# Two output tiles on LRU and S5 rows traced ahead of the end of the SSD stage, and half of w_out's SSD rows in another pool

## The chip, the cores and the metric

One core of one Trainium2 chip runs the whole program. The time is the device time of one execution in microseconds (us), as the median over runs. The engines are TensorE (PE, matmuls, with its weight loads as PEld), VectorE (DVE), ScalarE (ACT), GpSimd (POOL) and SyncE (SP), whose queue issues the DMAs here. Each engine works through its own instructions in a fixed order.

## What is computed

One step of a hybrid recurrent decoder layer, for 2048 prompt tokens and 64 sample tokens of width 1024:

```python
h = rmsnorm(x, norm_g) @ w_in            # split into z, xBC, dt, LRU, S5 columns
ssd = rmsnorm(ssd_scan(silu(conv(xBC)), dt, ...) * silu(z), ssd_norm_g)   # 16 heads, 4 groups, chunks of 128
lru = rg_lru(conv(...)) * gate           # 512 wide
s5  = glu(gelu(s5_scan(...))) * gate     # 512 wide
out = x + concat([ssd, lru, s5]) @ w_out # 2048 mix columns -> 1024
y   = rmsnorm(out, final_norm_g)
```

The outputs are y and the new states. All of it is held to float32 accuracy.

## The kernel before

The residual x is held on chip in four segments of 512 tokens and one of 64 sample tokens, each as two 16-bit tiles XH and XL (a high and a low part, 8 KB a partition) in the pool `xpool`, tag "xs", eight buffers. A float32 product is made as three 16-bit matmuls, high by high, high by low, low by high, with PSUM adding them up; `in_proj` (L247 to L249) does this for one block of 128 columns and one segment.

The stages follow one another: S5, LRU, and then SSD in four groups g = 0 to 3, each with the segments in the order 0, 1, (2, 4), 3. Within a segment there are four chunks of 128 tokens. A chunk needs the scores e (L524 to L531), its own y (L568 on e, L571 on the state hst carried from the chunk before), and its contribution to the state (L573, then hst L577 and L578). DVE adds y to x (L582), gates it (L655), and the rows go to a buffer `ysp` in the chip's memory (L383). Chunks 12 to 15, of segment 3, come last in a group. All rows of LRU and S5 were written to `ysp` long before.

The output stage multiplies the 2048 rows of y by w_out, 16 blocks of 128 rows: blocks 0 to 7 for SSD, 8 to 15 for LRU and S5. `w_out_rows` loads a block through a staging tile wo32 (two of them, L1144), takes a square sum on ACT (L1148) and small powers of two on DVE, and splits it into high and low on ACT (L1154) and DVE (L1155); two blocks share a tile `wo`. `w_out_scale` then finds one common scale for eight blocks, with a small matmul into ps_sc (L168), and rescales the tiles on DVE (L1168). `load_yt` reads 256 tokens of eight blocks' rows (y, L1182) and splits them into yt on ACT (L1186) and DVE (L1187). `out_part` makes 2 x 8 x 3 = 48 matmuls of 128x512 (L1175 to L1177) for a tile of 128 tokens, in two halves, each added into `res` by DVE (L1195).

The SSD rows need a norm over all of them: sqacc gathers their squares (L662), matmuls with ones sum them (L1302, L1303), and rstd and u0 follow. So for the first six tiles (NPRE) the LRU and S5 part comes first, 288 matmuls; then u0 is computed, and the rest of the tiles follows with both parts.

What sets the order on each engine is a scheduler that simulates the traced program: instructions are traced in the order of the code and are then placed by when they could start. Tiles get memory by pool: the output stage's pool `oa` takes the place of the SSD working pool (closed by `done` in the last segment of group 3), and `ob` takes the place of the pool `ssx`, closed by `sA.close()` after the last SSD row. Blocks are prepared as tiles of "xs" come free, which is during the last SSD group.

The functions around the change, with the lines that the profile names:

Of the kernel before, what the change touches and what calls it, by code (L numbers as in the profile page):

```python
# [8 lines left out]
F32 = mybir.dt.float32  # L9
F16 = mybir.dt.float16  # L10
# [32 lines left out]
def hymba_step_kernel(  # L43
# [577 lines left out]
                V.tensor_tensor(hv, hv, ps, op=ALU.add)  # L621
            S.dma_start(out=o_ssd_s[g, :, 4 * q:4 * q + 4], in_=hb)

    def ssd_group(sx, sp, g, done):
        blks = [2 * g, 2 * g + 1, 8 + g, 12 + g]
        ws = [WB[c0] for c0 in SB(g)]
        rows = [Row(k, unz[:, k:k + 1] if k < ZE else WB[k]) for k in (2 * g, 2 * g + 1)]
        tls = [Tail(b) for b in blks]
        H = None

        def channels(i, s):

            w, un, _ = ws[i]
            b = blks[i]
            raw = conv_raw(in_proj(w, s), un, s, tls[i], stS[:, b, :])
            if s == 3:
                w_ahead()
            x = seg_tile("xxbc"[i] + str(i % 2), "x", s, sx if i < 2 else sp, SG, 5 if i < 2 else 2)
            conv(x, raw, s, [col("sconv_w", 16 * j + b, hcols) for j in range(4)], col("sconv_b", b, hcols))
            th = seg_tile("th", "th", s, st)  # L640
            A.activation(out=th, in_=x, func=AF.Tanh)  # L641
            V.scalar_tensor_tensor(x, th, 1.0, x, op0=ALU.add, op1=ALU.mult)
            return x

        def gated(j, s, y):
            k = 2 * g + j
            s0, n = SEGS[s]
            if k < ZE:
                pz = seg_tile("pz", "pz", s, st)
                S.dma_start(out=pz, in_=zb[k, :, s0:s0 + n])  # L650
            else:
                pz = gate(in_proj(WB[k][0], s), WB[k][2], s)
                if s == 3:
                    w_ahead()
            V.tensor_tensor(y, y, pz, op=ALU.mult)  # L655
            if g == 0 and j == 0:
                sqacc[s] = sx.tile([128, SEGS[s][1]], F32, name="sqacc", tag=f"sqacc{s}", bufs=1)
                rows[j].add(s, y, sqacc[s])
            else:
                sq = sx.tile([128, SG], F32, name="sq", tag="sq", bufs=2)[:, :SEGS[s][1]]  # L660
                rows[j].add(s, y, sq)
                G.tensor_tensor(sqacc[s], sqacc[s], sq, op=ALU.add)  # L662

        for segs in SSD_ORD:
            xb = {s: [] for s in segs}
            for i in range(4):
                for s in segs:
                    xb[s].append(channels(i, s))
            for s in segs:
                x0, x1, BT, CT = xb[s]  # L670
                if s == 4:
                    ssd_sample(sp, g, (x0, x1), BT, CT)
                else:
                    for c in range(4 * s, 4 * s + 4):
                        H = ssd_chunk(sp, g, (x0, x1), BT, CT, c, H)
            if 3 in segs:
                S.dma_start(out=o_ssd_p[g], in_=H)
                done()
            for j in range(2):
                for s in segs:  # L680
                    gated(j, s, xb[s][j])


    t9 = const.tile([128, 4, 9], F32, name="t9")
# [449 lines left out]
    def w_out_rows(k0, nk):  # L1134


        tiles = []
        rb = tmp.tile([128, 8], F32, name="rb", tag="rb", bufs=3)
        for k in range(k0, k0 + nk):
            if (k - k0) % 2 == 0:  # L1140
                wo = xpool.tile([128, 2, 2, D], F16, name="wo", tag="xs")
            tiles.append(wo[:, (k - k0) % 2])
            w = wp.tile([128, D], F32, name="wo32", tag="w32", bufs=2)
            S.dma_start(out=w, in_=w_out[k * 128:(k + 1) * 128, :])  # L1144
            m = tmp.tile([128, 1], F32, name="o_m", tag="o_m")
            r = tmp.tile([128, 1], F32, name="o_r", tag="o_r", bufs=4)
            ng = col("ssd_norm_g", k) if k < 8 else 1.0
            A.activation(out=tiles[-1][:, 1, :].bitcast(BF16), in_=w, func=AF.Square, scale=ng, accum_out=m)  # L1148
            root_exponent(m, m)
            pow2_bits(r, m, 204)  # L1150
            pow2_bits(rb[:, k - k0:k - k0 + 1], r, 254)
            if k < 8:
                V.tensor_scalar(r, r, ng, None, op0=ALU.mult)
            A.activation(out=tiles[-1][:, 0, :], in_=w, func=AF.Copy, scale=r)  # L1154
            V.scalar_tensor_tensor(tiles[-1][:, 1, :], w, r, tiles[-1][:, 0, :], op0=ALU.mult, op1=ALU.subtract)  # L1155
        return tiles, rb
# [19 lines left out]
            P.matmul(ps, lhsT=h, rhs=w[:, 1, c], start=False, stop=False)  # L1176
            P.matmul(ps, lhsT=l, rhs=w[:, 0, c], start=False, stop=(k == nk - 1))  # L1177

    def load_yt(k0, t0, n):

        r = oa.tile([128, 8, 256], F32, name="y32", tag="y32", bufs=2)
        S.dma_start(out=r[:, :, :n], in_=ysp[k0:k0 + 8, :, t0:t0 + n].rearrange("k p t -> p k t"))  # L1182
        hl = (oa if k0 else ob).tile([128, 8, 2, 256], F16, name="yt", tag=f"yt{k0}", bufs=2)
        for k in range(8):
            c = rsc[:, k0 + k:k0 + k + 1]
            A.activation(out=hl[:, k, 0, :n], in_=r[:, k, :n], func=AF.Copy, scale=c)  # L1186
            V.scalar_tensor_tensor(hl[:, k, 1, :n], r[:, k, :n], c, hl[:, k, 0, :n], op0=ALU.mult, op1=ALU.subtract)  # L1187
        return [(hl[:, k, 0, :], hl[:, k, 1, :]) for k in range(8)]

    def out_part(tiles, yt, un, n, o, res):  # L1190
        for hf in range(2):
            c = slice(512 * hf, 512 * hf + 512)
            ps = bank(pmm, "mm", "ps_o")[:n]
            out_half(tiles, yt, n, o, ps, c)
            V.scalar_tensor_tensor(res[:n, c], ps, un, res[:n, c], op0=ALU.mult, op1=ALU.add)  # L1195
# [13 lines left out]
    def out_res(t0, n):  # L1209
        res = wp.tile([128, D], F32, name="res", tag="whl")  # L1210
        S.dma_start(out=res[:n], in_=x[t0:t0 + n])
        return res
# [7 lines left out]
    def pool(stack, name, side, bufs=1):  # L1220
        return stack.enter_context(tc.tile_pool(name=name, bufs=bufs, side=side, reuse_waits="tile"))
# [67 lines left out]
    sA, sB = ExitStack(), ExitStack()  # L1289
    sx = pool(sA, "ssx", "left")  # L1290
    sp = pool(sB, "ssw", "right", 2)
    for g in range(4):
        ssd_group(sx, sp, g, sB.close if g == 3 else (lambda: None))
    oq = ExitStack()
    oa = pool(oq, "outa", "right")
    rstd = const.tile([128, 17], F32, name="rstd")
# [12 lines left out]

    ob = pool(oq, "outb", "left")  # L1310
    NPRE = 6
    w1, rb1 = w_out_rows(8, 8)
    u1 = w_out_scale(w1, rb1, 8)
    w0, rb0 = w_out_rows(0, 8)
    pre = []
    for i in range(NPRE):
        if i % 2 == 0:
            yt1 = load_yt(8, 128 * i, 256)
        pre.append(out_res(128 * i, 128))
        out_part(w1, yt1, u1, 128, 128 * (i % 2), pre[i])  # L1320
    u0 = w_out_scale(w0, rb0, 0)
    rsu = tmp.tile([128, 17], F32, name="rsu", tag="rsu", bufs=1)
    V.tensor_scalar(rsu, rstd, u0, None, op0=ALU.mult)
    fg = ob.tile([128, D], F32, name="fg")
    S.dma_start(out=fg, in_=final_g.unsqueeze(0).to_broadcast([128, D]))
    fgs = ob.tile([128, 512], F32, name="fgs")
# [117 lines left out]
```

## Time and profile before

| | |
|---|---|
| median of 3 runs | 1679.58 us (1679.41 to 1679.8) |
| the profiled execution | 1682.5 us, span 1680.8 us |
| mean granted clock of PE | 0.971 |
| PE busy | 1587.2 us, 94% of the span, 9474 instructions |
| DVE, ACT, POOL busy | 1112.0, 858.2, 540.9 us |
| output matmuls (L1175 to L1177) | 3 x 512, 584.6 us |
| in_proj matmuls (L247 to L249) | 3 x 1280, 1474.6 us, overlapped with one another |

The profile is one execution of the program on the chip. A row of the timeline gives the start and the length of an operation (or of several alike) and, in brackets, how long its engine had been idle before it and what ended that. Matmuls follow each other faster than the length of one, because they are pipelined: their pace is read from starts. The granted clock of PE is a share of its full 2.4 GHz, so 0.50 is the level of 1.2 GHz. The stretch of interest is the last fifth: the SSD stage ends near 1319 us, the output stage runs to the end.

### The profile page before, as it was taken

Reading aid. Unit: us, or ns where it says so; the run is one execution under the profiler, and the core shown is the slowest. Engines: PE = TensorE matmul, PEld = TensorE weight load, DVE = VectorE, ACT = ScalarE, POOL = GpSimd, SP = SyncE. Lnnn points to the kernel's source line nnn. Section 1 sums busy time; section 2 is a strip of 40 time slices with the busy share of each in tenths; the row PEclk is TensorE's granted clock in tenths of the full one; section 3 lists DMA queues with packets and bytes.
Section 4 is the critical chain, followed back from the end, with each engine's and each line's share of the span. In section 5 each row is a group of like instructions: output and inputs, shape, how many; then the busy total and the mean of one; then the engine's idle time right before and its main releaser. Section 6 shows DMA issues by size and latency. Waiting matters only on the chain.

```text
span 1680.8 us, 26643 instructions
## 1 busy us (share of the span) xinstructions
PE 1587.2 (94%) x9474; PEld 820.9 (49%) x9474; DVE 1112.0 (66%) x2643; ACT 858.2 (51%) x1913; POOL 540.9 (32%) x822
## 2 busy tenths in 40 slices
PE   6899899898988999999999999999999799999998
PEld 3554544444434444455555555555555444444443
DVE  7844578997476665688878966687777725543332
ACT  7823434443697776666566646566765412322210
POOL 1213226774032111164557645454554100000000
PEclk9999799998989999999999999999999699999999
DMA  7412322322333442433434433242335522633100
GB/s 244 131 48 51 105 95 92 90 89 84 98 90 110 118 140 75 114 94 88 149 109 122 151 104 105 58 155 91 117 114 189 164 75 76 200 101 100 45 25 32
DMA packets 143942, 178.18 MB, mean 106 GB/s; under 512 B 66424, under 2 KB 92480, under 8 KB 143808
## 3 DMA queue, kind: packets, MB, share of 16 engines
q1 hardware_dynamic: 143808, 176.47, 34.4%
q8 instruction: 75, 1.23, 0.3%
q14 instruction: 59, 0.48, 0.1%
HBM read 126.57 MB, written 48.69 MB: 104 GB/s over the span
## 4 chain that ended last, share of the span: by engine, by line
PE 44%; DVE 7%; DMA 3%; ACT 3%; issue 2%; POOL 2%; SPq 0%; POOLq 0%; ACTq 0%; DVEq 0%
PE ps_o L1175 7%; PE ps_o L1176 7%; PE ps_o L1177 7%; PE ps_mm L248 5%; PE ps_mm L247 5%; PE ps_mm L249 5%; DVE x L355 3%; PE ps_y L568 1%; PE ps_s L573 1%; PE ps_y L571 1%; DMA ce<-eT 1%; PE ps_s L618 1%; DMA wo<-in_w_out_dram 1%; DVE e L531 1%; PE ps_tp L545 1%
## 5 line engine op out<-in xcount | busy, mean ns | idle before, releaser
L247 PE MATMUL ps_mm<-xh,whl 128*128 128x512 f16 x1280 | 492.0, 384 | 11.1 <-DVE pz L363 7.3
L249 PE MATMUL ps_mm<-xh,whl 128*128 128x512 f16 x1280 | 491.0, 384 | 0.9 <-DVE whl L206 0.9
L248 PE MATMUL ps_mm<-xl,whl 128*128 128x512 f16 x1280 | 491.6, 384 | 0.0
L248 PEld LDWEIGHTS <-whl 128*128 128x128 f16 x1600 | 155.6, 99 | 161.0 <-issue 29.4
L247 PEld LDWEIGHTS <-whl 128*128 128x128 f16 x1600 | 159.0, 101 | 145.3 <-issue 15.2
L249 PEld LDWEIGHTS <-whl 128*128 128x128 f16 x1600 | 156.1, 99 | 150.7 <-issue 14.2
L1175 PE MATMUL ps_o<-wo,yt 128*128 128x512 f16 x512 | 195.1, 381 | 5.2 <-ACT yt L1186 3.0
L355 DVE SCALAR_TENSOR_TENSOR x<-raw,hcols,x 128x512 f32<-128x512 f32 x192 | 173.6, 904 | 38.1 <-ACT x L353 35.9
L1176 PE MATMUL ps_o<-wo,yt 128*128 128x512 f16 x512 | 195.3, 381 | 0.0
L1177 PE MATMUL ps_o<-wo,yt 128*128 128x512 f16 x512 | 194.2, 380 | 0.0
L1186 ACT ACTIVATE yt<-y,rsc 128x256 f16<-128x256 f32 (+1 forms) x144 | 56.7, 477 | 109.9 <-PE ps_o L1177 81.1
L524 ACT ACTIVATE e<-bcq,acum 128x128 f32<-128x128 f32 (+1 forms) x272 | 85.7, 386 | 35.0 <-PE ps_y L568 32.7
L1347 ACT ACTIVATE yo<-res 128x1024 f32<-128x1024 f32 x16 | 16.8, 1049 | 154.6 <-DVE res L1195 154.5
L538 POOL TENSOR_TENSOR ce<-ce,x 128x512 f32<-128x512 f32 x60 | 81.5, 1364 | 42.5 <-DMA ce<-eT 34.3
L641 ACT ACTIVATE th<-x 128x512 f32<-128x512 f32 x64 | 40.1, 627 | 100.9 <-DVE x L355 100.6
L1195 DVE SCALAR_TENSOR_TENSOR res<-ps_o,rsu,res 128x512 f32<-128x512 f32 x32 | 24.0, 750 | 95.1 <-PE ps_o L1177 95.1
L1175 PEld LDWEIGHTS <-yt 128*128 128x128 f16 x512 | 50.4, 98 | 64.0 <-ACT yt L1186 3.3
L1176 PEld LDWEIGHTS <-yt 128*128 128x128 f16 x512 | 50.3, 98 | 63.1 <-issue 3.5
L363 DVE SCALAR_TENSOR_TENSOR pz<-th,ps_mm 128x512 f32<-128x512 f32 x64 | 43.6, 682 | 55.2 <-ACT th L362 54.7
L1177 PEld LDWEIGHTS <-yt 128*128 128x128 f16 x512 | 50.3, 98 | 60.9 <-issue 0.6
L531 DVE TENSOR_TENSOR e<-e,gm 128x512 f32<-128x512 f32 (+1 forms) x68 | 57.2, 841 | 28.5 <-POOL gm L530 23.8
L362 ACT ACTIVATE th<-ps_mm,sc_out 128x512 f32<-128x512 f32 x64 | 43.7, 682 | 61.9 <-PE ps_mm L249 61.3
(449 smaller groups left out, 3029.3 us busy)
## 6 DMA issues: line engine op xcount, KB each, us to landing
w<-in_w_blk_dram SPq DMA_DIRECT2D x40, 512.0 KB
bcq<-aT SPq DMA_DIRECT2D x64, 256.0 KB
y<-ysp SPq DMA_DIRECT2D x16, 1024.0 KB
ce<-eT SPq DMA_DIRECT2D x60, 256.0 KB
xt<-in_x_dram SPq DMA_DIRECT2D x16, 512.0 KB
ysp<-x SPq DMA_DIRECT2D x32, 256.0 KB
wo<-in_w_out_dram SPq DMA_DIRECT2D x16, 512.0 KB
res<-in_x_dram SPq DMA_DIRECT2D x16, 512.0 KB
```

Of the source, the lines that this page charges most:

```text
L247: P.matmul(ps[:, :n], lhsT=w[:, 0, k, :], rhs=XH[s][:, k, :], start=(k == 0), stop=False)
L248: P.matmul(ps[:, :n], lhsT=w[:, 0, k, :], rhs=XL[s][:, k, :], start=False, stop=False)
L249: P.matmul(ps[:, :n], lhsT=w[:, 1, k, :], rhs=XH[s][:, k, :], start=False, stop=(k == KD - 1))
L355: V.scalar_tensor_tensor(o, tap[j], w[j], o, op0=ALU.mult, op1=ALU.add)
L362: A.activation(out=th, in_=ps, func=AF.Tanh, scale=un2)
L524: A.activation(out=e[:n, h, :n], in_=bcq[:n, h, :n], func=AF.Relu, scale=-1.0, bias=acum[:n, c, 4 * g + h:4 * g + h + 1])
L531: V.tensor_tensor(e[:n, :, :n], e[:n, :, :n], gm.unsqueeze(1).to_broadcast([n, 4, n]), op=ALU.mult)
L538: G.tensor_tensor(ce[:, :, :n], ce[:, :, :n], CT[:, q0:q0 + n].unsqueeze(1).to_broadcast([128, 4, n]), op=ALU.mult)
L1175: P.matmul(ps, lhsT=h, rhs=w[:, 0, c], start=(k == 0), stop=False)
L1176: P.matmul(ps, lhsT=h, rhs=w[:, 1, c], start=False, stop=False)
L1177: P.matmul(ps, lhsT=l, rhs=w[:, 0, c], start=False, stop=(k == nk - 1))
L1186: A.activation(out=hl[:, k, 0, :n], in_=r[:, k, :n], func=AF.Copy, scale=c)
```

## The change

1. `ssd_group` takes a further function `mid`, called after the rows of segments 2 and 4. For group 3 it is `w1_ready`: blocks 8 to 15 of w_out are prepared and their common scale u1 is taken there, and no longer after the SSD stage.
2. Two tiles, i = 0 and 1, get their LRU and S5 part right after the last SSD group in the code, before the pool `oa` is opened. Their y and yt tiles are taken from "xs" (they get the buffers of x's third segment, XH and XL of 2).
3. Of w_out's SSD rows, blocks 0 to 3 take tiles of "xs" and blocks 4 to 7 take two tiles of `ob`, the pool in the memory of the closed `ssx`. Their scale u0 and rsu are computed before tile 4's LRU and S5 part, and no longer after tile 5's.

```diff
--- before.py
+++ after.py
@@ -621,7 +621,7 @@
                 V.tensor_tensor(hv, hv, ps, op=ALU.add)
             S.dma_start(out=o_ssd_s[g, :, 4 * q:4 * q + 4], in_=hb)
 
-    def ssd_group(sx, sp, g, done):
+    def ssd_group(sx, sp, g, mid, done):
         blks = [2 * g, 2 * g + 1, 8 + g, 12 + g]
         ws = [WB[c0] for c0 in SB(g)]
         rows = [Row(k, unz[:, k:k + 1] if k < ZE else WB[k]) for k in (2 * g, 2 * g + 1)]
@@ -679,6 +679,8 @@
             for j in range(2):
                 for s in segs:
                     gated(j, s, xb[s][j])
+            if 4 in segs:
+                mid()
 
 
     t9 = const.tile([128, 4, 9], F32, name="t9")
@@ -1138,7 +1140,8 @@
         rb = tmp.tile([128, 8], F32, name="rb", tag="rb", bufs=3)
         for k in range(k0, k0 + nk):
             if (k - k0) % 2 == 0:
-                wo = xpool.tile([128, 2, 2, D], F16, name="wo", tag="xs")
+                pl, kw = (xpool, dict(tag="xs")) if k0 or k < 4 else (ob, dict(tag="wo", bufs=2))
+                wo = pl.tile([128, 2, 2, D], F16, name="wo", **kw)
             tiles.append(wo[:, (k - k0) % 2])
             w = wp.tile([128, D], F32, name="wo32", tag="w32", bufs=2)
             S.dma_start(out=w, in_=w_out[k * 128:(k + 1) * 128, :])
@@ -1176,11 +1179,15 @@
             P.matmul(ps, lhsT=h, rhs=w[:, 1, c], start=False, stop=False)
             P.matmul(ps, lhsT=l, rhs=w[:, 0, c], start=False, stop=(k == nk - 1))
 
-    def load_yt(k0, t0, n):
-
-        r = oa.tile([128, 8, 256], F32, name="y32", tag="y32", bufs=2)
+    def load_yt(k0, t0, n, early=False):
+
+        if early:
+            r = xpool.tile([128, 8, 256], F32, name="y32", tag="xs")
+            hl = xpool.tile([128, 8, 2, 256], F16, name="yt", tag="xs")
+        else:
+            r = oa.tile([128, 8, 256], F32, name="y32", tag="y32", bufs=2)
+            hl = (oa if k0 else ob).tile([128, 8, 2, 256], F16, name="yt", tag=f"yt{k0}", bufs=2)
         S.dma_start(out=r[:, :, :n], in_=ysp[k0:k0 + 8, :, t0:t0 + n].rearrange("k p t -> p k t"))
-        hl = (oa if k0 else ob).tile([128, 8, 2, 256], F16, name="yt", tag=f"yt{k0}", bufs=2)
         for k in range(8):
             c = rsc[:, k0 + k:k0 + k + 1]
             A.activation(out=hl[:, k, 0, :n], in_=r[:, k, :n], func=AF.Copy, scale=c)
@@ -1289,8 +1296,24 @@
     sA, sB = ExitStack(), ExitStack()
     sx = pool(sA, "ssx", "left")
     sp = pool(sB, "ssw", "right", 2)
+    W1 = []
+
+    def w1_ready():
+        w1, rb1 = w_out_rows(8, 8)
+        W1[:] = w1, w_out_scale(w1, rb1, 8)
+
     for g in range(4):
-        ssd_group(sx, sp, g, sB.close if g == 3 else (lambda: None))
+        ssd_group(sx, sp, g, *((w1_ready, sB.close) if g == 3 else (lambda: None,) * 2))
+    w1, u1 = W1
+    pre = []
+
+    def pre_tile(i, yt1):
+        pre.append(out_res(128 * i, 128))
+        out_part(w1, yt1, u1, 128, 128 * (i % 2), pre[i])
+
+    yt1 = load_yt(8, 0, 256, True)
+    for i in range(2):
+        pre_tile(i, yt1)
     oq = ExitStack()
     oa = pool(oq, "outa", "right")
     rstd = const.tile([128, 17], F32, name="rstd")
@@ -1309,18 +1332,15 @@
 
     ob = pool(oq, "outb", "left")
     NPRE = 6
-    w1, rb1 = w_out_rows(8, 8)
-    u1 = w_out_scale(w1, rb1, 8)
     w0, rb0 = w_out_rows(0, 8)
-    pre = []
-    for i in range(NPRE):
+    for i in range(2, NPRE):
+        if i == NPRE - 2:
+            u0 = w_out_scale(w0, rb0, 0)
+            rsu = tmp.tile([128, 17], F32, name="rsu", tag="rsu", bufs=1)
+            V.tensor_scalar(rsu, rstd, u0, None, op0=ALU.mult)
         if i % 2 == 0:
             yt1 = load_yt(8, 128 * i, 256)
-        pre.append(out_res(128 * i, 128))
-        out_part(w1, yt1, u1, 128, 128 * (i % 2), pre[i])
-    u0 = w_out_scale(w0, rb0, 0)
-    rsu = tmp.tile([128, 17], F32, name="rsu", tag="rsu", bufs=1)
-    V.tensor_scalar(rsu, rstd, u0, None, op0=ALU.mult)
+        pre_tile(i, yt1)
     fg = ob.tile([128, D], F32, name="fg")
     S.dma_start(out=fg, in_=final_g.unsqueeze(0).to_broadcast([128, D]))
     fgs = ob.tile([128, 512], F32, name="fgs")
```

The scheduler makes of it the following. On PE, between chunk 13 (the first L573 row) and chunk 14, there stood twelve matmuls on sqacc; before:

```order
L573 MATMUL ps_s<-xw,bs 128x256
L520 MATMUL ps_g<-x 128x128
L1302 MATMUL ps_g<-ones,sqacc 128x1 x12
L568 MATMUL ps_y<-e,xdt 64x128 x2
L571 MATMUL ps_y<-ce,hst 64x128 x2
L568 MATMUL ps_y<-e,xdt 64x128 x2
L571 MATMUL ps_y<-ce,hst 64x128 x2
L573 MATMUL ps_s<-xw,bs 128x256
```

and after the change, nine of them and then the first output matmuls (line numbers are shifted, L1178 to L1180 are the lines of before L1175 to L1177):

```order
L573 MATMUL ps_s<-xw,bs 128x256
L1325 MATMUL ps_g<-ones,sqacc 128x1 x9
L1178 LDWEIGHTS yt
L1178 MATMUL ps_o<-wo,yt 128x512
L1179 LDWEIGHTS yt
L1179 MATMUL ps_o<-wo,yt 128x512
L1180 LDWEIGHTS yt
L1180 MATMUL ps_o<-wo,yt 128x512
```

Thirty-six of these stand ahead of chunk 14's first row, 6 more behind that row, 20 between chunk 14 and chunk 15, and 34 behind chunk 15. Then come the other sqacc matmuls, 115 output matmuls from tile 2 on, the ps_sc matmul of u0 and 77 output matmuls. Before, the ps_sc matmul stood behind all 288.

On DVE, up to chunk 13's x (L582) and the scores e of chunk 14 (L531; wo_14806 is a tile of block 4), before:

```order
L578 TENSOR_TENSOR hst<-hst,ps_s 128x256
L107 TENSOR_SCALAR o_r<-o_m 128x1
L1155 SCALAR_TENSOR_TENSOR wo<-wo_14806,o_r,wo 128x1024
L107 TENSOR_SCALAR rb<-o_r 128x1
L550 TENSOR_TENSOR xdt<-ps_tp,dt_all 128x256
L582 SCALAR_TENSOR_TENSOR x<-x,dpair,ps_y 128x128 x2
L1153 TENSOR_SCALAR o_r<-o_r,cols 128x1
L531 TENSOR_TENSOR e<-e,gm 128x512
```

and after the change, with the rescale of w1 by its scale:

```order
L107 TENSOR_SCALAR sc_out<-sc_out 128x1
L1169 TENSOR_SCALAR rb<-rb,sc_out 128x8
L1156 TENSOR_SCALAR o_r<-o_r,cols 128x1
L1171 TENSOR_SCALAR wo<-wo,rb 128x2048 x8
L582 SCALAR_TENSOR_TENSOR x<-x,dpair,ps_y 128x128 x2
L531 TENSOR_TENSOR e<-e,gm 128x512
L550 TENSOR_TENSOR xdt<-ps_tp,dt_all 128x256
L1158 SCALAR_TENSOR_TENSOR wo<-wo_14908,o_r,wo 128x1024
```

The rescale of w1 (before L1168, now L1171) stood behind the whole SSD stage and is now ahead of chunk 13's x and chunk 14's e; the tiles split next to it are now of blocks 2 and 3.

On SP, around the last SSD rows (ysp<-x), before (wo_14831 and wo_14843 are blocks 6 and 7):

```order
L537 DMA ce<-eT 128x512
L1144 DMA wo_14831<-in_w_out_dram 128x1024
L1144 DMA wo_14843<-in_w_out_dram 128x1024
L383 DMA ysp<-x 128x512 x2
L677 DMA out_dram<-hst 128x256
L1182 DMA y_14855<-ysp 128x8x256
L1182 DMA y_14982<-ysp 128x8x256
L1325 DMA fg<-in_final_g_dram 128x1024
L1329 DMA fgs<-in_final_g_dram 64x512 x2
L1182 DMA y_15109<-ysp 128x8x256
L1182 DMA y_15267<-ysp 128x8x256
```

and after the change (wo_14933 and wo_14945 are blocks 4 and 5, wo_14958 and wo_14970 blocks 6 and 7):

```order
L1147 DMA wo_14933<-in_w_out_dram 128x1024
L1147 DMA wo_14945<-in_w_out_dram 128x1024
L383 DMA ysp<-x 128x512
L677 DMA out_dram<-hst 128x256
L383 DMA ysp<-x 128x512
L1190 DMA y_14982<-ysp 128x8x256
L1190 DMA y_15132<-ysp 128x8x256
L1345 DMA fg<-in_final_g_dram 128x1024
L1349 DMA fgs<-in_final_g_dram 64x512 x2
L1190 DMA y_15267<-ysp 128x8x256
L1190 DMA y_15418<-ysp 128x8x256
L1147 DMA wo_14958<-in_w_out_dram 128x1024
L1147 DMA wo_14970<-in_w_out_dram 128x1024
```

Blocks 6 and 7 were loaded ahead of the last SSD rows and of every y load. Now they stand behind four y loads, two of LRU and S5 rows and two of SSD rows. The early y load of tiles 0 and 1 is not in this piece: it stands thirty rows ahead of it.

## Rows read from the trace of the kernel before

**Rows 1.** Table by stretch: length, busy time and instructions by engine, PE clock, DMA.

```profile
1270.00:1280.00 10.00, 10.00 (x91) 5.49 (x90) 7.64 (x9) 5.62 (x13) 4.55 (x7) 1.00 0.78 253
...
1294.00:1300.00 6.00, 4.23 (x35) 2.78 (x35) 5.16 (x17) 5.94 (x14) 1.51 (x3) 0.99 0.59 196
1300.00:1325.60 25.60, 17.08 (x90) 13.65 (x86) 20.16 (x56) 10.15 (x20) 10.34 (x12) 0.50 0.46 147
1325.60:1330.40 4.80, 4.80 (x12) 1.77 (x13) 4.21 (x14) 4.77 (x11) 0.00 (x0) 0.50 0.77 258
1330.40:1390.20 59.80, 59.80 (x278) 27.09 (x277) 21.28 (x47) 12.53 (x31) 0.00 (x0) 1.00 0.29 88
1390.20:1392.80 2.60, 0.33 (x3) 0.23 (x3) 2.25 (x9) 0.00 (x0) 0.00 (x0) 1.00 0.00 0
1392.80:1680.80 288.00, 280.35 (x1346) 127.68 (x1345) 116.64 (x267) 63.67 (x155) 0.00 (x0) 0.99 0.26 85
```

**Rows 2.** Waits of PE, 1280 to 1400 us: total us, times, longest.

```profile
PE ps_sc L168 <- DVE hst L578: 3.4, 1, 3.4
PE ps_o L1175 <- ACT yt L1186: 3.0, 1, 3.0
PE ps_o L1175 <- DVE wo L1168: 2.3, 1, 2.3
```

**Rows 3.** Chain of waits that ended last, 1294 to 1327 us: start, us, what.

```profile
1303.06 5.28 PE ps_g L1302 x24
...
1313.60 0.45 PE ps_y L571 x4
...
1319.08 5.84 DMA y<-ysp
```

**Rows 4.** Timeline of PE, 1245 to 1350 us: start, us, what, idle time before.

```profile
1248.61 0.44 PE L568 MATMUL ps_y<-e,xdt 128*64 128x128 f32 x4
...
1249.64 0.70 PE L573 MATMUL ps_s<-xw,bs 128*128 128x256 f32 x2
...
1299.31 0.44 PE L568 MATMUL ps_y<-e,xdt 128*64 128x128 f32 x4 [1.46 <-DVE o_m L116]
...
1301.00 1.22 PE L573 MATMUL ps_s<-xw,bs 128*128 128x256 f32 x2
...
1325.59 0.61 PE L1175 MATMUL ps_o<-wo,yt 128*128 128x512 f16 x1 [2.96 <-ACT yt L1186]
...
1348.81 0.38 PE L1175 MATMUL ps_o<-wo,yt 128*128 128x512 f16 x1
```

**Rows 5.** Timeline of DVE, 1245 to 1400 us.

```profile
1258.62 0.73 DVE L355 SCALAR_TENSOR_TENSOR x<-raw,hcols,x 128x512 f32<-128x512 f32 x1
...
1276.80 5.78 DVE L355 SCALAR_TENSOR_TENSOR x<-raw,hcols,x 128x512 f32<-128x512 f32 x3 [1.62 <-ACT x L353]
...
1315.20 1.28 DVE L1155 SCALAR_TENSOR_TENSOR wo<-wo,o_r,wo 128x1024 f16<-128x1024 f32 x1
...
1320.62 5.52 DVE L1168 TENSOR_SCALAR wo<-wo,rb 128x2048 f16<-128x2048 f16 x8
```

**Rows 6.** Timeline of POOL (GpSimd), 1245 to 1400 us.

```profile
1277.48 4.55 POOL L614 TENSOR_TENSOR hb<-hb,decs 128x1024 f32<-128x1024 f32 x2
...
1304.89 2.30 POOL L538 TENSOR_TENSOR ce<-ce,x 128x512 f32<-128x512 f32 x1 [0.85 <-DVE e L531]
```

**Rows 7.** Timeline of ACT, 1245 to 1400 us.

```profile
1259.40 1.15 ACT L1148 ACTIVATE wo<-wo,cols 128x1024 bf16<-128x1024 f32 x1 [0.46 <-DMA wo<-in_w_out_dram]
...
1325.03 3.31 ACT L1186 ACTIVATE yt<-y,rsc 128x256 f16<-128x256 f32 x8 [6.02 <-DMA y<-ysp]
1328.35 1.28 ACT L94 ACT_TABLE_LOAD   x1
```

**Rows 8.** Timeline of SP's DMA issues, 1245 to 1400 us.

```profile
1255.81 0.33 SPq L1144 DMA_DIRECT2D wo<-in_w_out_dram  x1
...
1329.56 28.26 SPq L1182 DMA_DIRECT2D y<-ysp  x5
```

## The prediction

> **What bounds the kernel now.** I read the table by stage first. TensorE (PE) is busy all of 1270 to 1280 us, 59.80 of 59.80 us from 1330.4 to 1390.2 and 280.35 of the last 288 us; between 1300 and 1325.6 it works 17.08 of 25.60 us, and at a granted clock of 0.50, the 1.2 GHz level [rows 1]. So the kernel is bound by matmuls almost everywhere, and the seam from the SSD stage to the output stage is where PE waits. Next the waits of PE at the seam: 3.4 us for VectorE's (DVE) hst L578, 3.0 us for ACT's yt L1186, and 2.3 us, 65 us later, for the rescaled SSD rows, wo L1168 [rows 2]. The chain of waits tells what is behind the first two: chunk 15's last matmul ends at 1313.60 + 0.45 = 1314.05, then its rows are gated and written, the first y load takes 5.84 us, and the first output matmul starts at 1325.59 [rows 3, 4]. During these 11.5 us PE has almost nothing to do, while 288 output matmuls on LRU and S5 rows, whose inputs have long been in memory, stand behind. The third wait is of the same kind: the u0 scale is computed when all 288 are done.
>
> The clock is the other loss. It falls to 0.50 at about 1300, after PE had been busy 4.23 of 6.00 us [rows 1] and had waited 1.46 us ahead of chunk 13 [rows 4]; it rises at 1330.4, 4.8 us after the output matmuls have begun to run without a gap. 12 matmuls there take 4.80 us (0.40 each), 278 after it 59.80 us (0.215 each) [rows 1].
>
> **The change, part by part.** The order of PE shows 96 of the 288 output matmuls in new places: 36 ahead of chunk 14, 26 between chunk 14's first matmul and chunk 15, 34 behind chunk 15. I follow PE to the first matmul of tile 2, which began at 1348.81 [rows 4].
>
> *Up to chunk 13.* New there: the y load (5.84 us, on SP ahead of bcq<-aTs; it waits for x's tile, read last by matmuls just ahead of 1248.61), eight ACT yt (3.31 us [rows 7]) and eight DVE yt (DVE does 47 operations of that stretch in 21.28 us, 0.45 each: 3.6 us). Moved away later: two w_out blocks, each 2 x 1.15 us of ACT [rows 7] and 1.28 us of DVE [rows 5]. ACT gains 1.3 us, DVE loses 1.0. The cover is in_proj, PE 10.00 of 10.00 us [rows 1], so I count nothing; if the cover were gone it would be DVE's 3.6 us (upper bound), below it nothing, since PE can't be more than busy. The scale of w1 now also stands here, nine small DVE operations (2.25 us in the 1390.2 row [rows 1]); about half falls into gaps, so chunk 13 starts at 1300.3 in place of 1299.31 (+1.0; bounds 0 and 2.25).
>
> *From 1300.3, half clock.* Chunk 13: 1.7 us (1299.31 to 1301.00) and L573 1.2 [rows 4]: 1303.2. Nine of the twelve sqacc matmuls, 18 of 24 passes of 5.28 us [rows 3], 4.0: 1307.2. The first 12 output matmuls as in the 1325.6 row, 4.8: 1312.0. There I take the clock to rise, after the same 4.8 us of gapless output matmuls as before.
>
> *Full clock.* Two paths lead to tile 2. By chunk 15: 50 more output matmuls x 0.215 = 10.75; chunk 14 with L573 1.03 + 0.70 = 1.73; chunk 15 1.03 (these from the in_proj stage, 1248.61 and 1249.64 [rows 4]): chunk 15 ends at 1325.5. From there to tile 2's first matmul it is the 11.5 us of before, less the L1155 of 1.28 us that stood between the gate operations on DVE [rows 5] and is now ahead of them, so 10.3: 1335.8. By PE's own work: 84 x 0.215 = 18.1, 2 x 1.73 for the two chunks, 2.0 for the other passes: 1335.6. They are even, so the 34 matmuls behind chunk 15 just cover its rows' way to memory and back. Tile 2 starts at 1335.8 where it was 1348.81: **13.0 us**.
>
> *w1's rescale* (eight L1168 at 5.52 us [rows 5], now L1171) stands on DVE ahead of chunk 13's x and of e for chunk 14. It can begin at about 1301 and end at 1306.5, in time for the first output matmul at 1307.2 and for chunk 14, which PE reaches 36 matmuls later at 1317.2. Counted as nothing; bounds 0 and the rival below.
>
> *u0 ahead of tile 4.* PE meets the ps_sc matmul 115 matmuls behind tile 2's start, at 1335.8 + 24.7 = 1360.5; 77 matmuls (16.6 us) follow it before the SSD rows are needed, and they hide the small operations and the rescale of 5.52 us: the 2.3 us wait goes. **2.3 us.** What is queued ahead of ps_sc: the last w_out blocks (k = 6, 7) now stand on SP behind four y loads and wait for a staging tile. ACT: tile 2's yt to 1338.6, two squares 2.3, a table load 1.3, eight yt 3.3, two splits 2.3: 1347.8; DVE's split 1.28, then the load of the last block 3.6 (1255.81 to 1259.40 [rows 7, 8]), while sixteen more yt, whose second y load goes out at about 1346 and takes 5.84, end by 1355; two squares 2.3 and eleven small operations at 0.25: 1360. That is even with 1360.5, so I count no wait, and what comes late here is lost one to one.
>
> **Sum.** 13.0 + 2.3 = 15.3 us. The profiled execution took 1682.5 us (span 1680.8), 2.9 over the median of 1679.58: 1682.5 - 15.3 = 1667.2, in the median **1664.3 us**. A difference of 0.2% (3.4 us) is what a measurement of this kernel can tell from none.
>
> **Rivals.**
>
> *The clock stays up.* With matmuls right behind chunk 13 it might never fall to 0.50. Then chunk 13, L573, the 18 passes and the 12 matmuls take 1.73 + 2.0 + 2.6 in place of 11.7, and tile 2 comes 5.4 us earlier: 1658.9. Against: it fell at 1300, before any of the moved matmuls stands in the order, and the stretch ahead of it is unchanged. Chance 0.13. The mirror belongs to the forecast: if gapless matmuls take twice 4.8 us to bring the clock back, another 2.4 us are lost, 1666.7.
>
> *Given back in part.* The rescale moves from 1320.6, where GpSimd was nearly quiet, to where GpSimd works 10.34 of 25.60 us [rows 1], with single operations of 2.30 [rows 6]. What such neighbours do to DVE stands at 1276.80: three L355 took 5.78 us beside two GpSimd operations of 4.55, one alone 0.73 [rows 5, 6]. If all of the 10.34 is added, the rescale ends at 1316.8, the first output matmul stands 9.6 us late, and chunks 14 and 15 with it: gain 5.7, 1673.9. If the one of 2.30 is added twice, it ends at 1311.1, 3.9 us late: gain 11.4, 1668.2. Late ps_sc (some us) or exposed yt (3.6) ends in the same place: 1667.6 to 1675.6. Chance 0.18, more of it at the near end, since several of those GpSimd operations are under 1 us.
>
> The Trainium skill, SBUF — State Buffer, "Who interferes with whom", speaks against the new place: tensor_scalar in a fast mode and a GpSimd operation share a port pair under an exclusive lock, and the later one fully blocks. By it the sum would be the late end of this rival, with each GpSimd operation added in full; the 1276.80 row agrees that DVE is held up (0.73 alone, 1.93 on average there), though for another kind of operation.
>
> *Hidden anyway.* Each matmul ahead of chunk 15 delays its rows, and with them tile 2's y load behind them on SP. If chunks 14 and 15 keep their old waits (3.4 us and more) between the new matmuls, or the order on the chip's queues makes the y load wait, the start of tile 2 slides back to 1347.7 or later: within 0.2%, 1676.2 to 1683. Against: in the order 34 matmuls stand behind chunk 15. Chance 0.04. That the matmuls aren't moved at all is excluded by the order.
>
> *Slower: ps_sc waits on the late blocks.* PE is in order, so 77 ready matmuls stand behind it. Five y loads were spread over 28.26 us on SP, 7.1 us from one to the next, with waits between them [rows 8]. Were the last two w_out blocks three such turns late, ps_sc would stand 21.2 us: 15.3 - 21.2, 5.9 us slower, 1685.5. It decides from 18.7 us of lateness. For it: blocks k = 6, 7 now stand behind four y loads, before behind none. Against: the turns of those loads are already in my 1360, and three more are not in the order. Chance 0.04.
>
> **Numbers.** Forecast (gain 12 to 18, 1661.6 to 1667.6) 0.61, clock up 0.13, part given back 0.18, hidden 0.04, slower 0.04. Faster 0.92, same 0.04, slower 0.04. The range 1658.0 to 1671.5 takes in the forecast, the clock rival and over half of the third case; the rest, some 0.16, is left out.
>
> **What would show it.** Right: the wait of PE for yt L1186 ahead of the output gone; 62 output matmuls ahead of chunk 15; half clock from 1300 to about 1312, 1.00 after; tile 2's first matmul near 1336; no wait for wo ahead of the SSD rows, ps_sc passed without a wait over 1 us. Wrong: a wait of the first output matmul for L1171 (contention), of tile 2 for yt (hidden), of ps_sc for DVE over some us (late blocks), a clock that does not rise until the chunks are over, or PE idle between 1250 and 1290.

## The result, and the profile after the change

The changed kernel took 1664.31 us in the median of 6 runs (1662.42 to 1671.17), the kernel before, beside it, 1679.69 us. The ratio is 0.9897, with a 95% interval of 0.9882 to 0.9912: faster, by 15.4 us between the medians and 17 us by the ratio. Two further sets of five runs, told below, gave 0.9886 (0.9867 to 0.9905) and 0.9891 (0.9874 to 0.9909). The forecast was 1664.3 us. The number came out almost to the digit; the parts of it did not, as the profile shows.

The profiled execution of the changed kernel took 1667.2 us (span 1665.5, mean granted clock 0.980 where it was 0.971). The stretches of the changed profile that answer to [rows 1], in the same columns (span, length, busy us and instructions by engine, PE's clock, DMA):

```profile
1280.00:1306.00 26.00, 23.13 (x152) 12.99 (x149) 19.21 (x37) 14.27 (x35) 12.96 (x15) 1.00 0.50 164
1306.00:1309.70 3.70, 3.61 (x37) 3.31 (x38) 3.70 (x9) 3.67 (x9) 3.63 (x5) 1.00 0.45 121
1309.70:1335.70 26.00, 26.00 (x152) 13.39 (x151) 17.77 (x39) 3.15 (x9) 8.62 (x8) 1.00 0.42 134
1335.70:1377.00 41.30, 41.30 (x197) 18.91 (x196) 31.67 (x86) 22.57 (x45) 0.00 (x0) 1.00 0.50 157
1377.00:1660.00 283.00, 280.68 (x1349) 127.76 (x1346) 111.63 (x257) 63.67 (x155) 0.00 (x0) 1.00 0.26 85
```

The columns between length and clock are PE, its weight loads, DVE, ACT and GpSimd (POOL). From 1306 to 1377 PE is all but without a gap: 3.61 of 3.70, 26.00 of 26.00 and 41.30 of 41.30 us. Where the kernel before had 30 us at 0.50 there is 1.00 throughout. In front of it, though, PE is busy 23.13 of 26.00 us, and the waits of PE from 1240 to 1400 us (columns as in [rows 2]) are other ones:

```profile
PE ps_s L618 <- DVE hb L621: 2.1, 1, 2.1
PE ps_s L618 <- POOL bm L612: 1.6, 1, 1.6
PE ps_g L520 <- ACT gm L529: 0.6, 2, 0.4
PE ps_y L568 <- DVE e L531: 0.2, 1, 0.2
```

All three long waits of [rows 2] are gone. Two at L618, the sample chunk's contribution to the state, are new, 3.8 us together (ahead of 1269.39 and of 1290.25). The wait of 1.46 us ahead of chunk 13 [rows 4] is 0.17 now. Then the timeline of PE, for the places of [rows 4]:

```profile
1253.58 0.70 PE L573 MATMUL ps_s<-xw,bs 128*128 128x256 f32 x2
...
1306.09 0.44 PE L568 MATMUL ps_y<-e,xdt 128*64 128x128 f32 x4 [0.17 <-DVE e L531]
...
1309.69 0.38 PE L1178 MATMUL ps_o<-wo,yt 128*128 128x512 f16 x1
...
1335.73 0.39 PE L1178 MATMUL ps_o<-wo,yt 128*128 128x512 f16 x1
...
1360.57 0.28 PE L168 MATMUL ps_sc<-w_mx,ones 128*128 128x1 f32 x2
```

The first row is the same instruction as the one at 1249.64 in [rows 4], in code that the change doesn't touch: it stands 3.9 us later. In these 3.9 us are two more short falls of the clock in this one execution, near 962 and 1235 us, about 1.7 us each. Counted from that row, chunk 13 begins after 52.5 us (before: 49.7), and tile 2 comes 29.6 us behind chunk 13 (before: 49.5). Tile 2 has gained 17.0 us, not 13.0. From the first row to the end of the span it is 411.9 us, where it was 431.2: 19.2 us less, more than the medians of this first comparison show. The last row is u0's ps_sc: passed without a wait.

DVE in the same profile: the early yt, w1's rescale, e of chunk 14, the operation that ps_sc waits for, and w0's rescale:

```profile
1260.07 4.63 DVE L1194 SCALAR_TENSOR_TENSOR yt<-y,rsc,yt 128x256 f16<-128x256 f32 x8 [1.68 <-ACT yt L1193]
...
1306.72 7.77 DVE L1171 TENSOR_SCALAR wo<-wo,rb 128x2048 f16<-128x2048 f16 x8
...
1314.93 0.68 DVE L531 TENSOR_TENSOR e<-e,gm 128x512 f32<-128x512 f32 x1
...
1358.67 0.16 DVE L177 TENSOR_TENSOR w_mx<-w_mx 128x1 f32<-128x1 f32 x1
...
1362.76 5.39 DVE L1171 TENSOR_SCALAR wo<-wo,rb 128x2048 f16<-128x2048 f16 x8
```

The rescale that took 5.52 us [rows 5] takes 7.77 us in its new place, and 5.39 where GpSimd is quiet. GpSimd's neighbours there:

```profile
1307.25 1.68 POOL L538 TENSOR_TENSOR ce<-ce,x 128x512 f32<-128x512 f32 x1
...
1310.82 1.80 POOL L538 TENSOR_TENSOR ce<-ce,x 128x512 f32<-128x512 f32 x1 [1.19 <-DMA ce<-eT]
```

### The profile page after: what moved, and what is told of

Its sections match the earlier page's. It is cut to its first block, busy times and chain, and to the rows that moved or that the text cites. A ratio compares the mean times of both kernels' runs of the same rounds, so it can differ in the third digit from the quotient of the medians.

```text
span 1665.5 us, 26647 instructions
## 1 busy us (share of the span) xinstructions
PE 1580.5 (95%) x9474; PEld 814.7 (49%) x9474; DVE 1114.9 (67%) x2643; ACT 858.8 (52%) x1913; POOL 542.2 (33%) x822
## 4 chain that ended last, share of the span: by engine, by line
PE 44%; DVE 8%; ACT 3%; issue 2%; DMA 2%; POOL 1%; SPq 0%; POOLq 0%; ACTq 0%; DVEq 0%
PE ps_o L1180 7%; PE ps_o L1178 7%; PE ps_o L1179 7%; PE ps_mm L248 6%; PE ps_mm L247 6%; PE ps_mm L249 6%; DVE x L355 3%; PE ps_y L568 1%; PE ps_s L573 1%; PE ps_y L571 1%; PE ps_s L618 1%; DVE e L531 1%; PE ps_tp L545 1%; DVE x L642 1%; PE ps_o L1212 1%
## 5 line engine op out<-in xcount | busy, mean ns | idle before, releaser
L1178 PE MATMUL ps_o<-wo,yt 128*128 128x512 f16 x512 | 193.9, 379 | 0.0
L1180 PE MATMUL ps_o<-wo,yt 128*128 128x512 f16 x512 | 193.7, 379 | 0.0
L538 POOL TENSOR_TENSOR ce<-ce,x 128x512 f32<-128x512 f32 x60 | 82.5, 1381 | 44.5 <-DMA ce<-eT 35.6
L1178 PEld LDWEIGHTS <-yt 128*128 128x128 f16 x512 | 50.2, 98 | 60.1
L1180 PEld LDWEIGHTS <-yt 128*128 128x128 f16 x512 | 50.1, 98 | 60.2 <-issue 0.2
L531 DVE TENSOR_TENSOR e<-e,gm 128x512 f32<-128x512 f32 (+1 forms) x68 | 55.9, 821 | 27.7 <-POOL gm L530 22.0
```

What stands on the lines that cost most here:

```text
L531: V.tensor_tensor(e[:n, :, :n], e[:n, :, :n], gm.unsqueeze(1).to_broadcast([n, 4, n]), op=ALU.mult)
L538: G.tensor_tensor(ce[:, :, :n], ce[:, :, :n], CT[:, q0:q0 + n].unsqueeze(1).to_broadcast([128, 4, n]), op=ALU.mult)
L1178: P.matmul(ps, lhsT=h, rhs=w[:, 0, c], start=(k == 0), stop=False)
```

## Experiments

Each is set against the kernel before on the same chip, with ratios and 95% intervals. "After the row at 1249.64" means the first row of PE above: positions are counted from it, since what lies ahead of it varies by some us between executions.

### The changed kernel again

No edit.

> The changed kernel once more, for its profile and its spread. Theory (the gaps of PE are filled, and thereby the clock does not fall): as before, about 15 us under the kernel before, granted clock 1.00 from chunk 13 to tile 2, about 29.6 us from chunk 13's first matmul to tile 2's first, and again two waits of PE at L618, for bm and hb, of 1 to 2 us each in the in_proj stage. Rival (the clock stayed up by luck in the one profile): clock 0.50 somewhere between chunk 13 and the first dozen output matmuls, that stretch 35 us or more, the time about 5 us longer than in a profile without it.

1662.45 us, ratio 0.9886 (0.9867 to 0.9905). Its profile (timeline of PE, the two anchors):

```profile
1249.66 0.70 PE L573 MATMUL ps_s<-xw,bs 128*128 128x256 f32 x2
...
1301.30 0.44 PE L568 MATMUL ps_y<-e,xdt 128*64 128x128 f32 x4 [0.18 <-DVE e L531]
```

This execution stands level with that of before at 1249.64 (0.02 us apart). Chunk 13 follows after 51.6 us, and the clock is 1.00 from there to tile 2. The two waits at L618 are 2.1 and 0.9 us. What the one profile showed came again. From the row to the end it is 20.1 us less than before.

> The changed kernel a third time, beside yt_first and on the same chip. Theory: ratio to before 0.988 to 0.991, clock 1.00 from chunk 13 to tile 2 in its profile, as in the other two. Rival (the clock's stay is luck): a fall to 0.50 in that stretch.

1663.01 us, ratio 0.9891 (0.9874 to 0.9909), again 1.00 from chunk 13 on, waits of 2.1 and 1.6 us, chunk 13 after 52.6 us, tile 2 29.7 us behind it, and 19.1 us less than before from the row to the end. The theory holds in all three executions.

### Without the early tiles

```diff
-    yt1 = load_yt(8, 0, 256, True)
-    for i in range(2):
-        pre_tile(i, yt1)
-    for i in range(2, NPRE):
+    for i in range(NPRE):
```

> The change without its second part: no tile ahead of the SSD stage's end, w1 and its scale early and u0 ahead of tile 4 as in the change. Theory (the gain is matmuls in PE's gaps): all but the u0 term is lost, 2.2 us under the kernel before, ratio 0.9987, and the clock falls to 0.50 near chunk 13 or soon behind it until the output matmuls have run some 5 us. Rival (the gain is the clock, and what keeps it up is the other order of DVE and ACT ahead of chunk 13): the clock stays at 1.00 and 5 us or more are gained without the tiles, ratio 0.997 or less.

1676.05 us, ratio 0.9964 (0.995 to 0.9977). The clock falls at 1300.5, as the theory has it, and but for some 3 us it is at 0.50 until 1324.5. But 6 us are gained, more than the u0 term; the theory's 0.9987 was missed. The chain of waits tells how (start, us, what):

```profile
1298.56 4.44 DVE wo L1171 x5
...
1303.28 2.42 DVE wo L1171 x3
...
1314.12 6.40 DMA y<-ysp
...
1321.24 0.61 PE ps_o L1178
```

The y load goes out at 1314.12, where it was 1319.08 [rows 3], 4.2 us earlier when counted from the row at 1249.64 (here at 1248.90): blocks 4 to 7 of w_out, whose splits stood on DVE between the chunks and the gate, are now prepared later. Of the 4.2 us, 1.9 are there already at chunk 15's L573, and the other 2.4 come behind it. The prediction had this side effect of the third part of the change only as 1.28 us. The rows also show w1's rescale on the path, 4.44 and 2.42 us ahead of chunk 14: in its new place it has a price, which only other work for PE can hide. The tiles themselves are worth the rest, from 0.9964 down to the three ratios of the change: 11 to 13 us.

### Only w1 early, only u0 early, u0 late

w1's rows and scale early in the kernel before, and nothing else:

```diff
+    def w1_ready():
+        w1, rb1 = w_out_rows(8, 8)
+        W1[:] = w1, w_out_scale(w1, rb1, 8)
...
+    w1, u1 = W1
...
-    w1, rb1 = w_out_rows(8, 8)
-    u1 = w_out_scale(w1, rb1, 8)
```

> The kernel before with w1's rows and scale early (the first part of the change alone). It splits what tiles_back gained. Theory (w1's rescale and the splits leave the tail behind chunk 15, where they stood between the gate and the y load): the y load goes out 2 us or so earlier against chunk 15, ratio to before 0.997 to 0.9985, the wait for the rescaled SSD rows is still there. Rival (tiles_back's gain is u0 and the spread of runs): the time before, ratio 0.999 to 1.001.

1681.74 us, ratio 1.0004 (0.9993 to 1.0015): the rival's number, nothing gained. Its chain:

```profile
1308.20 3.64 DMA wo<-in_w_out_dram
...
1314.24 1.46 DVE wo L1157
...
1316.30 0.53 DVE wo L1157
```

Blocks 6 and 7 are loaded in the middle of the chunks, and their splits (L1157 here) stand on DVE in front of the gate, one of them waiting for the 3.64 us load. So w1's early place gains nothing by itself, and what the run before this one gained beyond u0 is put down to the later place of blocks 4 to 7. That is a difference of runs: no run has this place alone.

u0 ahead of tile 4 in the kernel before, and nothing else:

```diff
     for i in range(NPRE):
+        if i == NPRE - 2:
+            u0 = w_out_scale(w0, rb0, 0)
...
-    u0 = w_out_scale(w0, rb0, 0)
```

> The kernel before with u0 and rsu ahead of tile 4's part and nothing else. Theory: the 2.3 us wait for the rescaled rows goes and nothing else changes, ratio 0.9986. Rival (ps_sc then waits for its scales, with the ready matmuls behind it): a wait of PE at L168 takes its place, ratio 0.9995 to 1.002.

1678.61 us, ratio 0.9979 (0.9968 to 0.9989), 3.5 us with an interval of 1.8 to 5.4 that holds the 2.3. The wait is gone and no other stands between 1340 and 1400 us. Another 1.3 us come ahead of it: the first output matmul stands 74.7 us behind the row at 1249.64 (here at 1251.28), where it was 76.0. This run also says something of the clock. Its order on PE up to chunk 15 is that of before, and yet the sqacc matmuls between chunk 13 and 14 ran in half the time (5.28 us in [rows 3]):

```profile
1303.53 2.84 PE L1302 MATMUL ps_g<-ones,sqacc 128*128 128x1 f32 x24 [0.45 <-ACT gm L529]
```

Here the clock fell only at 1306, behind them: 55.0 us after the row, where it had been 50.3. The order of the work on PE alone does not fix the place of the fall.

And the change with u0 back behind tile 5:

```diff
     for i in range(2, NPRE):
-        if i == NPRE - 2:
-            u0 = w_out_scale(w0, rb0, 0)
...
         pre_tile(i, yt1)
+    u0 = w_out_scale(w0, rb0, 0)
```

> The change with u0 and rsu back behind tile 5's LRU and S5 part. Theory (u0's place is worth its wait): 2.2 us over the changed kernel, ratio to before about 0.991, and a wait of PE for the rescaled rows of 2 to 2.5 us is back. Rival (PE passes ps_sc late anyway, or the rescale is hidden): no wait, the time of the changed kernel.

1668.31 us, ratio 0.9912 (0.9894 to 0.993). The wait is back at the first SSD matmul:

```profile
1378.66 0.38 PE L1178 MATMUL ps_o<-wo,yt 128*128 128x512 f16 x1 [2.28 <-DVE wo L1171]
```

2.28 us, as the theory said. The difference of the ratios is 2.5 us from 0.9897 and up to 4.4 from the others; in this profile the clock is also at 0.50 for 3.4 us behind the wait, which costs another 1.7 us. Behind the same wait in the kernel before it stayed at 1.00.

### The same matmuls, but only behind chunk 14

`with behind(x)` has what is traced inside it placed only behind the instruction x; LAST[14] is chunk 14's matmul on the state (L573 of the change).

```diff
+    with behind(LAST[14]):
         for i in range(2):
             pre_tile(i, yt1)
```

> The change, but the early tiles' matmuls may only stand behind chunk 14's last matmul (18 ahead of chunk 15, 78 behind it; none between chunk 13 and chunk 14). Theory (the clock holds because matmuls stand right behind chunk 13): the clock falls to 0.50 between chunk 13 and chunk 15 as it did without the tiles, PE waits 4 us or so ahead of chunk 14 again, and the time is 6 to 10 us over the change, ratio to before 0.992 to 0.995. Rival (any place of the 96 matmuls does, PE makes up for it behind chunk 15): clock at 1.00, under 3 us over the change.

1676.09 us, ratio 0.9958 (0.9943 to 0.9973): 10 to 12 us given back, a little more than the theory had. A stretch of its table, then three rows of PE's timeline:

```profile
1310.00:1322.00 12.00, 5.59 (x32) 3.70 (x32) 11.21 (x18) 0.95 (x3) 5.55 (x5) 0.57 0.26 80
```

```profile
1306.67 0.44 PE L569 MATMUL ps_y<-e,xdt 128*64 128x128 f32 x4 [0.17 <-DVE e L532]
...
1316.33 0.70 PE L569 MATMUL ps_y<-e,xdt 128*64 128x128 f32 x4 [5.25 <-DVE e L532]
...
1344.72 0.39 PE L1179 MATMUL ps_o<-wo,yt 128*128 128x512 f16 x1
```

From 1310 to 1322 PE works 5.59 of 12.00 us, most of it at 0.50. Chunk 14 waits 5.25 us for e, which stands on DVE behind w1's rescale. From chunk 13 to tile 2 it is 38.1 us, where the change needs 29.6 and the kernel before 49.5: 8.5 us are given back in this stretch. The rest stands ahead of chunk 13, which comes 55.65 us after the row: in this one profile the clock was at 0.50 from 1287.5 to 1294.5, ahead of any moved matmul. Four of the nine runs took 1672.3 us or less, so not all of the 10 to 12 us need be the place of the matmuls. The 8.5 us are: the 36 ahead of chunk 14 cover the rescale.

### Matmuls that do no work

To see what the clock is worth by itself, 48 matmuls whose sums nobody reads were put into the gaps of the kernel without early tiles:

```diff
+    with behind(LAST[13]):
+        for i in range(3):
+            ps = bank(pmm, "mm", "ps_d")
+            for j in range(16):
+                P.matmul(ps, lhsT=w1[j % 8][:, 0, 0:128], rhs=w1[j % 8][:, 0, 512:1024], ...)
```

> The kernel without early tiles (the run tiles_back), with 48 matmuls of 128x512 in the gaps behind chunk 13, 14 and 15 whose sums nobody reads: work added, none moved. Theory (what fills the gaps keeps the clock, whatever it is): clock 1.00 from 1290 to the first output matmuls, chunks 14 and 15 and the first dozen output matmuls at full speed, 3 to 6 us under tiles_back, ratio to before 0.993 to 0.9947. Rival (only the saved work counts, added matmuls cost their time or nothing): the time of tiles_back or up to 5 us over it, ratio 0.9964 to 0.9995.

1682.18 us, ratio 1.0002 (0.9991 to 1.0014): slower than without them by 6 us, even over the rival's range. The clock fell at 1300.6, ahead of the first of them, was back at 1304 and stayed at 1.00 until 1321, 73 us after the row at 1249.64; without them it fell again after 65 us. So they do seem to keep it up, but they are on the chain themselves:

```profile
1301.88 5.90 PE ps_d L1313 x22
...
1309.44 4.32 PE ps_d L1313 x20
...
1317.45 6.01 DMA y<-ysp
...
1324.18 0.61 PE ps_o L1179
```

Counted from the row (here at 1247.97), the y load goes out after 69.5 us, and after 65.2 without the added matmuls. While it was under way PE was idle and the clock fell again (the first output matmul took 0.61 us). What the added matmuls cost on this chain is more than the clock gave back, so the run doesn't price the clock by itself. In the change PE itself is the bound from chunk 13 on, and there the 1.00 counts: in yt_first2 below the clock was at 0.50 for 3.4 us behind chunk 13, and from chunk 13 to tile 2 it took 31.3 us in place of 29.7. What the change gains first is the work that was moved.

### Where the early yt stand

Three kernels move the early y load and yt. Behind the sample chunk's e on DVE:

```diff
+    with behind(LAST["e"]):
         yt1 = load_yt(8, 0, 256, True)
```

> The change, but the early yt stand on DVE behind the sample chunk's e (before: ahead of its xdt). Theory (the two waits at L618 in the in_proj stage, 3.0 and 3.8 us in sum, come from eight yt on DVE ahead of the sample chunk): the waits go for the most part, 2 to 3 us under the change, ratio to before 0.985 to 0.988. Rival (the eight yt only move and delay the channels of the last segment instead): chunk 13 no earlier, the time of the change.

1664.31 us, ratio 0.9896 (0.9877 to 0.9914), the rival's number. The waits have only changed place:

```profile
PE ps_s L620 <- DVE hb L623: 1.7, 1, 1.7
...
PE ps_tp L546 <- DVE x L644: 1.4, 1, 1.4
```

Chunk 13 follows after 53.5 us, no earlier than in the change; in this profile the clock was also at 0.50 from 1288 to 1291.5.

Behind the channels of the last segment (L642 of the fourth block):

```diff
+    with behind(LAST[3, 3]):
         yt1 = load_yt(8, 0, 256, True)
```

> The change, but the early yt stand on DVE behind the last segment's channels (L642 of the fourth): only 20 matmuls fit ahead of chunk 14, 20 ahead of chunk 15, 56 behind it. Theory (early waits as in yt_behind_e): the in_proj stage as in the kernel before, chunk 13 some 2 us earlier than in the change, and since PE has the same work in the gaps, 1 to 3 us under the change. Rival (DVE is the bound around chunk 13, and yt there delays e and x of the chunks): chunk 14 waits for e, PE idles again, the change's time or up to 5 us over it.

1672.02 us, ratio 0.9946 (0.9931 to 0.9962), the rival again. Chunk 12 comes 1.1 to 2.1 us earlier than in the change, but chunk 13 does not: it begins 52.2 us after the row (here at 1252.83). Only 20 matmuls fit ahead of chunk 14, the clock is at 0.50 from 1302 to 1315, and ACT and DVE are late for the scores. First chunk 13's row, then waits of PE:

```profile
1305.01 0.70 PE L569 MATMUL ps_y<-e,xdt 128*64 128x128 f32 x4 [0.58 <-DVE sc_m L115]
```

```profile
PE ps_g L521 <- ACT gm L530: 2.2, 3, 1.6
...
PE ps_y L569 <- DVE e L532: 1.0, 1, 1.0
```

And ahead of w1's rows, in the buffers of x's first segment, free long before:

```diff
     def w1_ready():
+        Y1.append(load_yt(8, 0, 256, True))
         w1, rb1 = w_out_rows(8, 8)
...
-    yt1 = load_yt(8, 0, 256, True)
+    yt1 = Y1[0]
```

> The change, but the early y load and its yt are traced ahead of w1's rows, so that they get the buffers of x's first segment, which come free over 50 us earlier; the order of PE from chunk 12 on is that of the change. Theory (the waits of PE at L618, 3.0 and 3.8 us in the two profiles, are the price of eight yt on DVE between the chunks of the (2, 4) segments): they shrink to 1 us or less, chunk 13 stands 1 to 3 us earlier against 1249.65, ratio to before 0.986 to 0.989 and below that of the run beside it. Rival (some other work of DVE takes their place, as with yt_behind_e): the waits stay, no difference from the run beside it.

1657.59 us, ratio 0.9864 (0.9842 to 0.9885). DVE makes the eight yt 90 us earlier, between other work:

```profile
1164.54 1.28 DVE L1194 SCALAR_TENSOR_TENSOR yt<-y,rsc,yt 128x256 f16<-128x256 f32 x3 [0.68 <-ACT yt L1193]
...
1166.91 2.08 DVE L1194 SCALAR_TENSOR_TENSOR yt<-y,rsc,yt 128x256 f16<-128x256 f32 x5 [1.08 <-ACT yt L1193]
```

and PE's waits shrink to

```profile
PE ps_g L520 <- ACT gm L529: 0.6, 2, 0.4
PE ps_s L618 <- DVE hb L621: 0.5, 1, 0.5
PE ps_y L568 <- DVE e L531: 0.2, 1, 0.2
```

with the anchors

```profile
1246.95 0.70 PE L573 MATMUL ps_s<-xw,bs 128*128 128x256 f32 x2
...
1295.91 0.44 PE L568 MATMUL ps_y<-e,xdt 128*64 128x128 f32 x4 [0.18 <-DVE e L531]
...
1325.61 0.39 PE L1178 MATMUL ps_o<-wo,yt 128*128 128x512 f16 x1
```

Chunk 13 follows after 49.0 us (before 49.7, the change 51.6 to 52.6), and tile 2 29.7 us later, as in the change: some 3 us are gained, ahead of chunk 13.

> yt_first once more, on whatever chip comes. Theory (its gain over the change is the 2 to 3 us of waits that are gone, and the rest of the 5 us seen was spread): ratio to before 0.986 to 0.9885, waits of PE at L618 under 1 us in the profile. Rival (the gain was the luck of that chip): ratio 0.989 or more, the waits back.

1660.6 us, ratio 0.9866 (0.9848 to 0.9884), and no wait at L618 in the profile. The theory holds twice: this version is below both kernels, below the change by 3 to 6 us in the ratios, whose intervals still overlap a little, and by 1.6 to 3.8 us in the profiles from the row to the end. It differs from the change by the order of two calls, which also shifts the preparation of w_out's blocks somewhat.

## Why the prediction was right

**The direction, the place of the gain and its order of size are right; that the figure agrees to a us is luck.** One step failed in the kernel's favour (5.9 us from chunk 13 to tile 2), another against it (1.0 to 2.0 us ahead of chunk 13), and with both the gain is 19 to 20 us. That is what the three profiles show from the row to the end (19.1 to 20.1 us); that the first comparison of medians shows 15.4 lies within the spread of the runs. By the prediction's own steps:

*Up to chunk 13* it counted 1.0 us, and nothing for the early yt, with DVE's 3.6 us as the upper bound, because in_proj keeps PE busy 10.00 of 10.00 us. Measured: 2.0, 2.8 and 3.0 us in the three profiles. The cover was read from the wrong row. PE's share being full in that stretch did not mean that a late DVE was harmless. The eight yt (4.63 us) stood on DVE in front of the sample chunk's xdt. On ACT the squares of a w_out block (L1151) waited 1.91 us for them, with the sample chunk's bs (L552) behind them, of which GpSimd makes bm; and DVE's hb came late too. PE's L618 needs both. So the sign that the prediction names, PE idle between 1250 and 1290, was there. The run yt_first takes the load and the yt away from this place, and the loss goes. This is the mis-sized term. The 1.0 us itself, which stood for w1's scale, is not seen: with that scale in the same place, yt_first reaches chunk 13 0.7 us earlier than the kernel before.

*From 1300.3, half clock* is the step that failed. The prediction took the fall at 1300 as a fixture, since "the stretch ahead of it is unchanged". It was not: the 1.46 us wait ahead of chunk 13 had shrunk to 0.17, and the waits at L618 were new. In all three profiles chunk 13, the passes and the first dozen output matmuls ran at 1.00, which is worth the 5.4 us that the first rival gave it. From chunk 13 to tile 2 it is 29.6 us in place of the 35.5 of the sum. That only_u0 has its fall elsewhere shows why the ground was weak; what decides the moment of a fall no run settles. What they do show: without output matmuls between chunk 13 and chunk 14 it fell, by tile 2, in every profile (the kernel before, tiles_back, only_u0, only_w1, late_fill). In yt_behind_x and idle_matmuls, with 20 and 22 there, it had fallen before the first of them (at 1301.8 and 1300.6). With 36 there it stayed up in six of seven, and in the seventh, yt_first2, it was at 0.50 for 3.4 us. So the rival that had 0.13 is what happened in mechanism. Its time of 1658.9 was missed by the loss ahead of chunk 13 and by the spread.

*Tile 2* came 17.0 us earlier (13.0 forecast) when counted from the first row of PE; the 3.9 us of that execution ahead of it hide this in the profile's total, whose difference is 15.3. The ratios, 0.9886 to 0.9897, stand for 17 to 19 us, and 15.3 us (0.9909) lies inside the first of the three intervals, outside the second and at the edge of the third.

*Full clock, two paths.* Right to some tenths: 29.6 us less chunk 13 and the passes is what 96 matmuls, two chunks and the other passes take. Tile 2's y load came just in time. The prediction calls this way that of chunk 15's rows "to memory and back"; the load reads LRU and S5 rows and only stands behind chunk 15's rows on SP:

```profile
1328.86 1.15 SPq L1190 DMA_DIRECT2D y<-ysp  x2
```

```profile
1334.89 3.30 ACT L1193 ACTIVATE yt<-y,rsc 128x256 f16<-128x256 f32 x8 [5.68 <-PE ps_g L1325]
```

The y load is issued at 1328.86 and yt begins at 1334.89; PE, with no gap, begins tile 2 at 1335.73.

*w1's rescale* was hidden as said, but it did grow, by 2.3 us beside GpSimd operations of 1.68 and 1.80 us. The prediction's bound of 10.34 us was far too wide. It grew by about half of the 4.8 us that GpSimd worked beside it (0.60, 1.68, 0.74 and 1.80), and GpSimd's L538 was slowed too (1.28 us at 1253 us in the kernel before). The Trainium skill (SBUF — State Buffer, "Who interferes with whom") says that whichever of the two issues first holds the shared ports for its whole instruction and that the other is fully blocked. The trace agrees that the two hold each other up. The forecast's late end had DVE as the blocked one each time; here both paid, and no run separates their shares. That it cost nothing is due to the 36 matmuls: e of chunk 14 was done at 1315.6, PE came at 1317.55. Where they were taken away (late_fill) PE waited 5.25 us for it.

*u0* was right in size and place: ps_sc 24.8 us behind tile 2's start for 24.7, and the row it waits for done at 1358.83, so 1.7 us to spare where the sum had half a us. The rival on the slower side, ps_sc waiting for late blocks, had its ground but not its size (in yt_behind_x ps_sc did wait, 0.2 us). Nor did the y load keep tile 2 back, as the rival on the hidden gain had it.

*A term that the sum lacked*: blocks 4 to 7 no longer stand on DVE between the chunks and the gate. In tiles_back the y load came 4.2 us earlier, and only_w1, without that part, gained nothing; in the change it is hidden, since PE's own work is as long.

## What to carry to other kernels

Work that is ready and waits behind a seam can be worth nearly its own length when it is put into the seam (here 17.0 us for 96 matmuls of 0.215), but where in the seam matters: the same 96 matmuls one chunk later gave back 8.5 us between chunk 13 and tile 2, and 10 to 12 us in the medians. Its preparation has to be placed with as much care as the work: look at what stands behind it on every engine's queue, not at how busy the engine to be covered is, and let it take the memory that comes free first. And count positions from a row in untouched code, since two executions can differ by 4 us ahead of it.

## Not expected of the hardware

With the same order of work on PE, the clock's fall moved from 50.3 to 55.0 us behind the same row between two profiles. With 48 matmuls without use the granted clock stood at 1.00 over 16 us, and the kernel was still 6 us slower: on a chain that waits for DVE and a DMA, work that is added to hold the clock can cost more than the clock gives back.
